# Hybrid SSD + S5 decoder step on one core: S5 coefficient and rotation products moved from GpSimd to VectorE, S5 state split into two 64-row halves

## The chip, the cores and the metric

The kernel runs on one core of one Trainium2 chip. The metric is the device time of one execution in microseconds, the lower the better. The kernel before was timed in three runs.

## The reference, cut to what matters

One decoder layer is computed for 1024 prompt tokens and 8 samples of 4 tokens (1056 columns in all). The input is normed and projected; one half of the projection feeds a Mamba-2 branch (SSD), the other an S5 branch; both are gated, joined by an output projection, and followed by a gate and a final norm. The change lies in the S5 branch, which has 64 groups of 16 channels, each driving a 64-dimensional complex diagonal state:

```python
delta = jnp.exp(log_dt)[:, None]
ab = exp(lambda * delta)                        # complex, per group and state
bb = ((ab - 1) / lambda) * b                    # complex input matrix
bu = einsum('btgh,gph->btgp', u, bb)
x  = associative_scan(x_t = ab * x_{t-1} + bu_t)   # from h0
y  = einsum('btgp,ghp->btgh', x_re, c_re) - einsum('btgp,ghp->btgh', x_im, c_im) + d * u
```

(In the reference the complex products are written out in real and imaginary parts.)

## The kernel before

All work is feature-major: 128 features on the partitions, the 1056 tokens in three chunks of 352 columns. `dense` (L159 to L169, its matmuls on L167) makes one 128-row tile of a projection as 8 blocks of 3 products each (high and low parts of weight and input), so 24 matmuls of 352 columns a chunk and 72 a tile. In the text these are the "dense matmuls". Weights come through one raw buffer `wr` and are split by ScalarE (L73) and VectorE (L76, `wl<-wr,wh`).

The S5 branch is made in two stages.

- **Coefficients** (`s5_coef_base` L306, `s5_coef_batch` L428). 16 batches of 4 groups. A batch makes three matrices in SBUF and stores them to DRAM in `md`: the output matrix `op` (c times powers of a: three VectorE operations of 128x576, L453 to L455), the input matrix `wt` (powers of a times b: three GpSimd operations of 128x512, L478 to L480, then four transposes `wp` on TensorE and a copy by ScalarE), and a Toeplitz matrix that goes from matmuls `kp` by a small VectorE operation `ks` through `kd` in DRAM into `md` (eight DMAs for four batches, L471, on SyncE's queue). `op`, `wt`, `ks` and `bs` have two buffers each. The batches are interleaved with the dense tiles of u, two a tile.
- **Scan** (`s5_batch` L633). 16 batches of 4 groups, that is 2 pairs. A batch loads `u8`, `mm` (its slice of `md`) and `h8`; TensorE makes the inputs `vr`, `vi` (64 output rows for each group, two groups side by side on 128 partitions, L650); a table of rotations `cr`, `sr` is the complex product of two small tables (`cmul` on L660: six operations of 128x256 on GpSimd, with `sst` as scratch); VectorE rotates `vr`, `vi`, runs four scans (L674), rotates back and writes the state `sst`. In `sst` a group has its real parts on partitions 0 to 63 and its imaginary parts on 64 to 127, while the scan has the two groups of a pair there, so four VectorE operations of 64x256 write it (L682, L686). TensorE then adds two products of 128 rows a group into `yp`: Toeplitz times u (L693) and `op` times state (L694); ScalarE applies gelu (L695). The batches are interleaved with the 12 convolution tiles (`conv_tile`, three VectorE operations `acc` of 128x1080 each) and the dt tile.

After that come the SSD stage (with z_b tiles as filler), z_a, the output projection, the GLU and the gate. The order of instructions on each engine is fixed when the kernel is built: the scheduler places them by a simulated timeline, so a change in one stage can move the dense matmuls of others. Each engine runs its own list strictly in order.

Of the kernel before, what the change touches and what calls it, by code (L numbers as in the profile page):

```python
# [7 lines left out]
F32 = mybir.dt.float32  # L8
# [16 lines left out]
CW = 352  # L25
# [9 lines left out]
def hymba_ssd_s5_kernel(  # L35
# [10 lines left out]
    s5h: bass.AP,  # L46
# [90 lines left out]
    md = dt_("md", 128, 64, 3, 128)  # L137
# [33 lines left out]
    # 1 / sqrt(mean of squares + eps) of the tokens of a chunk, on every partition  # L171
# [5 lines left out]
    def rstd_tok(sqs, n):  # L177
        """sqs: feature-major squares [128, CW]; the result [token, group of tokens]."""
        sp = psa("nsp")
        qt = sqs[0].shape[1] // 4  # L180
        for j in range(4):
            for i, q in enumerate(sqs):
                PE.matmul(out=sp[0:qt, j:j + 1], lhsT=q[:, qt * j:qt * j + qt], rhs=ones[:, 0:1],
                          start=(i == 0), stop=(i == len(sqs) - 1))
        v, y, t = (nw_p.tile([128, 4], F32, tag=q, name=q, bufs=b)[0:qt] for q, b in (("nv", 2), ("ny", 3), ("nt", 2)))
        ts(v, sp[0:qt, 0:4], 1.0 / n, EPS, ALU.mult, ALU.add)
        ts(y.bitcast(I32), v.bitcast(I32), 1, None, ALU.logical_shift_right)
        ts(y.bitcast(I32), y.bitcast(I32), -1.0, float(0x5F3759DF), ALU.mult, ALU.add)
        for _ in range(3):
            mul(t, v, y)  # L190
            stt(t, y, -0.5, t, ALU.mult, ALU.mult)
            stt(y, t, 1.5, y, ALU.add, ALU.mult)
        return y

    def rstd_bcast(y):
        """on every partition: a PSUM tile [128, CW]"""
        qt = y.shape[0]
        rb = psb("nrb")[:, 0:4 * qt]
        for j in range(4):
            PE.matmul(out=rb[:, qt * j:qt * j + qt], lhsT=y[:, j:j + 1].to_broadcast([qt, 128]),  # L200
                      rhs=ident[0:qt, 0:qt], start=True, stop=True)
        return rb

    def rstd_wide(y, n):
        """y, in place = 1 / sqrt(mean of y over n + 4 eps) on every partition; a Newton step polishes the root"""
        w = y.shape[1]
        sb, v = psb("nsb")[:, 0:w], ev("nv", w)
        PE.matmul(out=sb, lhsT=ones, rhs=y, start=True, stop=True)
        act(v, sb, AF.Identity, scale=1.0 / n, bias=eps4)
        act(y, v, AF.Ln)  # L210
        act(y, y, AF.Exp, scale=-0.5)
        mul(sb, v, y)
        stt(sb, sb, -0.5, y, ALU.mult, ALU.mult)
        stt(y, sb, 1.5, y, ALU.add, ALU.mult)
        return y
# [90 lines left out]
    def s5_coef_base():  # L306
# [57 lines left out]
        # rotation tables (partition = (g2, p), free = (pair, c))  # L364
# [9 lines left out]
        # a^4 h0 of the sample group  # L374
# [11 lines left out]
        # P[k] = a^k (rows 0-63), i a^k (rows 64-127), k = 0..8  # L386
# [13 lines left out]
        # f = (a - 1) / lambda  # L400
# [16 lines left out]
        # Z: f over -f  # L417
# [10 lines left out]
    def s5_coef_batch(b):  # L428
        cf, cf2, P, Z = cfc["p"], cfc["p2"], cfc["P"], cfc["Z"]
        g0, g1 = GB * b, GB * b + GB  # L430
        if b % 4 == 0:
            cfc["bc"] = row("bc")[:, 0:1024]
            for q2 in range(2):
                dma(out=cfc["bc"][64 * q2:64 * q2 + 64], in_=s5bc[:, b // 4])
            # b-bar (rows 0-63), minus b-bar (rows 64-127), re and im
            bn = cfc["bc"].rearrange("p (b t r x) -> p b t r x", b=4, t=2, r=2)[:, :, 0]
            zz = row("bz")[:, 0:1024].rearrange("p (r b g h) -> p r b g h", r=4, b=4, g=GB)
            n4 = lambda i: bn[:, :, i].rearrange("p b (g h) -> p b g h", h=16)
            f4 = lambda i: Z[:, i, g0:g0 + 16].rearrange("p (b g) -> p b g", b=4).unsqueeze(3).to_broadcast([128, 4, GB, 16])
            cmul(zz[:, 0], zz[:, 1], n4(0), n4(1), f4(0), f4(1), zz[:, 2], zz[:, 3])  # L440
            cfc["bz"] = zz
# [6 lines left out]
        # O[(ri, p), g, k, h] = (Re; -Im) of c a^k  # L448
# [7 lines left out]
        # rows 64-127 of P hold i a^k: Re(i c a^k) = -Im(c a^k)  # L456
        dms(out=md[:, g0:g1, 2], in_=op[:, :, 1:9].rearrange("p g k h -> p g (k h)"))
# [15 lines left out]
        # W[(s, h), g, (ri, p)] = (Re; Im) of a^(7-s) f b, built transposed  # L473
# [4 lines left out]
        mul(wt, x8(0), b8_(0), G)  # L478
        mul(w2, x8(1), b8_(1), G)
        sub(wt, wt, w2, G)  # L480
# [47 lines left out]
    def dt_tile():  # L528
# [11 lines left out]
        # w high | w low on 32 partitions; summed by the transposes to [token, chunk, head]  # L540
# [21 lines left out]
        # log1p(y) = ln(u) - ((u - 1) - y) / u with u = 1 + y rounded  # L562
# [6 lines left out]
        # sums over the tokens of a chunk or a sample row: up to each token, and of all of them  # L569
# [17 lines left out]
        # the 32 sample tokens three times over the partitions  # L587
# [45 lines left out]
    def s5_batch(b):  # L633
# [20 lines left out]
        sst = s5.tile([128, NB, 137], F32, tag="sst", name="sst")  # L654
        tc_, td = (sst.rearrange("p g c -> p (g c)")[:, 256 * i:256 * i + 256].rearrange("p (j c) -> p j c", c=128)
# [4 lines left out]
        cmul(v4(cr), v4(sr), b16(0), b16(1), b1(0), b1(1), v4(tc_), v4(td), G)  # L660
# [27 lines left out]
        yt = s51.tile([128, NB, 136], F32, tag="yt", name="yt")
# [10 lines left out]
    def ssd_mt(k, g, L, cb):  # L699
        """masked decay times C B, [s][head][l]"""  # L700
        mt = sdc["p"].tile([128, 8, 128], F32, tag="ab", name="ab", bufs=ABB)[0:L, :, 0:L]
        if k < 8:
            dma(out=mt, in_=acs_d[16 * k + 8 * g:16 * k + 8 * g + 8].partition_broadcast(L))
        else:
            dma(out=mt, in_=acs_s[8 * g:8 * g + 8].rearrange("e b s -> e (b s)").partition_broadcast(L))
        cbm = sdc["p"].tile([128, 128], F32, tag="cbm", name="cbm")[0:L, 0:L]
        mul(cbm, cb[0:L, 0:L], causal if k < 8 else cs[0:32, C_SMASK:C_SMASK + 32])
        for e in range(8):
            act(mt[:, e], mt[:, e], AF.Relu, scale=-1.0, bias=tok[0:L, 0, k, 8 * g + e:8 * g + e + 1])
        act(mt, mt, AF.Exp, scale=-1.0)  # L710
        mul(mt, mt, cbm.unsqueeze(1).to_broadcast([L, 8, L]))
        return mt
# [65 lines left out]
    def sample_prep():  # L778
# [3 lines left out]
        for g in range(2):  # L782
            # the 32 tokens three times over the partitions: high, high, low parts of B against high, low, high of x
# [77 lines left out]
    s5fin = cc.tile([128, 64], F32, name="s5fin")  # L861
# [158 lines left out]
    # scaled by the final norm and stored, while the next chunk is under way  # L1020
# [47 lines left out]
def _layout(i):  # L1068
# [15 lines left out]
    def tiles(w):  # L1084
# [30 lines left out]
    a["s5h"] = f(h.transpose(0, 3, 2, 1).reshape(128, 64, 8))  # L1115
# [17 lines left out]
         ("o_s5p", (128, 64)), ("o_s5s", (128, 2, 32, 8))]  # L1133


def _outputs(r):
# [9 lines left out]
    s5p = r["o_s5p"].reshape(2, 64, 64).transpose(0, 2, 1).reshape(2, 1, 1, 64, 64)  # L1146
# [18 lines left out]
```

## Time and profile before

| what | value |
|---|---|
| median of 3 runs | 1073.57 us (1072.02 to 1079.29) |
| profiled execution, span | 1074.0 us |
| mean granted TensorE clock | 0.972 |
| TensorE busy | 1018.8 us (95%) |
| VectorE busy | 760.1 us (71%) |
| ScalarE busy | 457.1 us (43%) |
| GpSimd busy | 307.0 us (29%) |

The span runs from the first to the last instruction. No other time of the profiled execution is given; its span is 0.4 us above the median of the runs, so that what lies around it is not told apart from the scatter of the runs, and sums made in the trace are read as times of a run. The matmuls overlap each other (one of 352 columns is shown as 0.32 us long, while the next starts 0.16 us later), so a busy TensorE is not a full one. The shares are means over stages that differ: by the slices of the page, VectorE is near 100% busy from about 110 to 200 us and from 275 to 430 us, and 30 to 50% in the last third.

### The profile page before, as it was taken

The page shows a single profiled execution, that of the slowest core. Times are in us where ns is not written, and L with a number is a line of the kernel's source. Part 1 is how long each engine was busy: PE and PEld are TensorE (multiplying, and loading weights), DVE is VectorE, ACT ScalarE, POOL GpSimd, SP SyncE. Part 2 cuts the span into 40 slices and gives each one's busy share as a digit, 9 for nine tenths or more (in the row PEclk, how much of TensorE's full clock was granted, in tenths as well). Part 3 has the DMA queues.
Part 4 walks back from the last instruction along what each step waited for, and adds up shares of the span by engine and source line. Part 5 has one row for each costly group of instructions (what it writes and reads, how often), then busy time and mean ns, then how long its engine had stood idle before and what let it go on. Part 6 is the DMA issues. An engine that isn't in the chain of part 4 may idle for free.

```text
span 1074.0 us, 17756 instructions
## 1 busy us (share of the span) xinstructions
PE 1018.8 (95%) x6608; PEld 962.8 (90%) x6608; DVE 760.1 (71%) x1460; ACT 457.1 (43%) x926; POOL 307.0 (29%) x385
## 2 busy tenths in 40 slices
PE   7999887899999989999999999999999999999995
PEld 7899776699989889987788899899999999999995
DVE  5779999776999999478789785667333334455466
ACT  7534134437444441575554567423233333324321
POOL 0600689643345433124443221000000002221221
PEclk9899998899999999999999999999999999999997
DMA  9526377652234455446653211698522322322232
GB/s 319 197 74 175 106 206 202 181 192 97 100 123 155 153 165 193 148 145 205 203 168 120 70 60 54 219 307 281 184 92 81 110 90 87 105 102 79 81 120 102
DMA packets 112486, 157.12 MB, mean 146 GB/s; under 512 B 13584, under 2 KB 88464, under 8 KB 112400
## 3 DMA queue, kind: packets, MB, share of 16 engines
q1 hardware_dynamic: 83376, 136.46, 39.2%
q10 hardware_dynamic: 29024, 19.54, 5.8%
q8 instruction: 52, 0.85, 0.3%
q14 instruction: 34, 0.28, 0.1%
HBM read 109.49 MB, written 50.67 MB: 149 GB/s over the span
## 4 chain that ended last, share of the span: by engine, by line
PE 47%; DVE 21%; DMA 8%; issue 5%; ACT 4%; SPq 1%; DVEq 0%; ACTq 0%
PE psd L167 40%; DVE acc L88 3%; DMA gr<-gd 2%; DVE sst L76 2%; DVE ta L76 2%; DVE tb L76 2%; DVE wl L76 2%; DMA hp_d<-xl 1%; DVE ui L674 1%; DVE op L76 1%; ACT L73 1%; DVE ur L674 1%; DMA wr<-wall 1%; PE yd L717 1%; DVE x L88 1%
## 5 line engine op out<-in xcount | busy, mean ns | idle before, releaser
L167 PE MATMUL psd<-n_h,wh 128*128 128x352 f32 x864 | 289.4, 335 | 0.4 <-DVE zt L88 0.4
L167 PE MATMUL psd<-n_h,wl 128*128 128x352 f32 x864 | 288.5, 335 | 0.0
L167 PE MATMUL psd<-n_l,wh 128*128 128x352 f32 x864 | 287.4, 333 | 0.0
L167 PEld LDWEIGHTS psd<-n_h,wh 128*128 128x128 f32 x864 | 166.6, 193 | 6.5 <-issue 3.6
L167 PEld LDWEIGHTS psd<-n_l,wh 128*128 128x128 f32 x864 | 166.6, 193 | 5.4 <-issue 4.6
L167 PEld LDWEIGHTS psd<-n_h,wl 128*128 128x128 f32 x864 | 166.1, 192 | 5.9 <-issue 5.5
L76 DVE TENSOR_TENSOR wl<-wr,wh 128x1024 fp32r<-128x1024 f32 (+1 forms) x64 | 81.7, 1277 | 46.4 <-ACT wh L73 45.6
L73 ACT ACTIVATE wh<-wr 128x1024 fp32r<-128x1024 f32 (+2 forms) x65 | 67.0, 1031 | 87.3 <-PE psd L167 78.3
L76 POOL TENSOR_TENSOR ssq<-ssq,xl 128x352 f32<-128x352 f32 x21 | 21.5, 1024 | 276.9 <-ACT xl L73 276.9
L76 POOL TENSOR_TENSOR sst<-r,r 128x256 f32<-128x256 f32 x64 | 52.0, 834 | 72.0 <-PE yp L694 41.5
L167 PE MATMUL psd<-ya_h,wh 128*128 128x352 f32 x192 | 63.5, 333 | 6.8 <-DVE xl L76 6.5
L73 ACT ACT_TABLE_LOAD x39 | 50.0, 1283 | 37.1 <-DVE acc L88 30.8
L73 ACT ACTIVATE ab<-ab,tok 128x128 f32<-128x128 f32 (+1 forms) x144 | 42.8, 380 | 49.2 <-DMA ab<-acs_d 29.7
L167 PE MATMUL psd<-ya_l,wh 128*128 128x352 f32 x192 | 63.3, 330 | 0.0
L167 PE MATMUL psd<-ya_h,wl 128*128 128x352 f32 x192 | 63.2, 330 | 0.0
L167 PE MATMUL psd<-yb_l,wh 128*128 128x352 f32 x192 | 62.2, 324 | 0.0
L167 PE MATMUL psd<-yb_h,wl 128*128 128x352 f32 x192 | 62.0, 323 | 0.0
L167 PE MATMUL psd<-g_l,wh 128*128 128x352 f32 x192 | 61.8, 322 | 0.0
L167 PE MATMUL psd<-g_h,wh 128*128 128x352 f32 x192 | 61.8, 322 | 0.0
L167 PE MATMUL psd<-g_h,wl 128*128 128x352 f32 x192 | 61.8, 322 | 0.0
L167 PE MATMUL psd<-yb_h,wh 128*128 128x352 f32 x192 | 61.7, 321 | 0.0
L167 PE MATMUL psd<-hg_h,gwl 128*128 128x400 f32 (+1 forms) x144 | 46.7, 324 | 0.0
(315 smaller groups left out, 2350.9 us busy)
## 6 DMA issues: line engine op xcount, KB each, us to landing
wr<-wall SPq DMA_DIRECT2D x68, 512.0 KB, 3.3
mm<-md SPq DMA_DIRECT2D x16, 768.0 KB, 6.2
ab<-acs_d SPq DMA_DIRECT2D x16, 512.0 KB, 4.5
ud<-ub ACTq DMA_DIRECT2D x8, 576.0 KB, 3.7
u<-ud SPq DMA_DIRECT2D x16, 288.0 KB, 3.3
gd<-yt SPq DMA_DIRECT2D x16, 272.0 KB, 4.4
gr<-gd SPq DMA_DIRECT2D x8, 544.0 KB, 5.1
x<-xT SPq DMA_DIRECT2D x24, 176.0 KB, 5.3
```

The source lines that it names most:

```text
L73: return S.activation(out=out, in_=in_, func=func, **kw)
L76: return (eng or V).tensor_tensor(out=out, in0=a, in1=b, op=op)
L88: return V.scalar_tensor_tensor(out=out, in0=a, scalar=s, in1=b, op0=op0, op1=op1)
L167: PE.matmul(out=ps, lhsT=a[:, ko + k, :], rhs=b, start=(i == 0), stop=(i == 3 * K - 1))
L674: V.tensor_tensor_scan(out=u[:, j], data0=cb["mag8"][:, j0 + j:j0 + j + 1].to_broadcast([128, 128]), data1=u[:, j], initial=0.0, op0=ALU.m ...
L717: PE.matmul(out=yd[64 * (e % 2):64 * (e % 2) + 64, e // 2], lhsT=x1[:, e], rhs=mt[:, e], start=True, stop=True)
```

## The change

- In `s5_coef_batch` the three `wt` operations of a batch run on VectorE instead of GpSimd.
- In `s5_batch` the six operations of `cmul` that make `cr`, `sr` run on VectorE instead of GpSimd.
- The state `sst` is kept as it comes from the scan: partitions are (half, p), the half being the group of the pair, and real and imaginary parts stand side by side in the free dimension. It is written by two VectorE operations of 128x256 instead of four of 64x256.
- The product `op` times state of a group becomes two matmuls of 64 rows (real, imaginary) on the half of the partitions where the group lies; the two groups of a pair use different halves and write different PSUM tiles. In fp32 each matmul is two instructions: a batch has 16 of 64 rows instead of 8 of 128 rows.
- `op` is stored in a DRAM tensor of its own, `od`, by four DMAs a batch instead of one (on ScalarE's queue), and loaded into its own tile `om`; `mm` shrinks from 768 to 512 KB. `h8` is loaded from `s5ha`, and the input `s5h` goes away. The layout of one output follows.

```diff
-    md = dt_("md", 128, 64, 3, 128)
+    md = dt_("md", 128, 64, 2, 128)
+    od = dt_("od", 2, 64, 32, 2, 128)
...
-        dms(out=md[:, g0:g1, 2], in_=op[:, :, 1:9].rearrange("p g k h -> p g (k h)"))
+        for q in range(2):
+            for ri in range(2):
+                dms(out=od[q, :, g0 // 2:g1 // 2, ri],
+                    in_=op[64 * ri:64 * ri + 64, q::2, 1:9].rearrange("p g k h -> p g (k h)"))
...
-        mul(wt, x8(0), b8_(0), G)
-        mul(w2, x8(1), b8_(1), G)
-        sub(wt, wt, w2, G)
+        mul(wt, x8(0), b8_(0))
+        mul(w2, x8(1), b8_(1))
+        sub(wt, wt, w2)
...
-        mm = s5.tile([128, NB, 3, 128], F32, tag="mm", name="mm")
+        mm = s5.tile([128, NB, 2, 128], F32, tag="mm", name="mm")
         dma(out=mm, in_=md[:, g0:g0 + NB])
-        tm, wv, om = mm[:, :, 0], mm[:, :, 1], mm[:, :, 2]
-        h8 = s5.tile([128, NB, 8], F32, tag="h8", name="h8")
-        dma(out=h8, in_=s5h[:, g0:g0 + NB])
+        tm, wv = mm[:, :, 0], mm[:, :, 1]
+        om = s5.tile([128, NJ, 2, 128], F32, tag="om", name="om")
+        dma(out=om, in_=od[:, :, j0:j0 + NJ].rearrange("q p j r c -> (q p) j r c"))
+        h8 = s5.tile([128, 2, NJ, 8], F32, tag="h8", name="h8")
+        dma(out=h8, in_=s5ha[:, :, j0:j0 + NJ])
...
-        cmul(v4(cr), v4(sr), b16(0), b16(1), b1(0), b1(1), v4(tc_), v4(td), G)
+        cmul(v4(cr), v4(sr), b16(0), b16(1), b1(0), b1(1), v4(tc_), v4(td))
...
-        for q in range(2):
-            sub(s2[0:64, :, q, 9:137], ta[64 * q:64 * q + 64], tb[64 * q:64 * q + 64])
+        sub(sst[:, 0, :, 9:137], ta, tb)
         mul(ta, ui, cr)
         mul(tb, ur, sr)
+        add(sst[:, 1, :, 9:137], ta, tb)
...
-        for h in range(NB // 2):
-            yp = psb("yp")[:, 0:272].rearrange("p (g c) -> p g c", c=136)
-            for i in range(2):
-                g = 2 * h + i
-                PE.matmul(out=yp[:, i], lhsT=tm[:, g], rhs=u8[:, g, 0:136], start=True, stop=False)
-                PE.matmul(out=yp[:, i], lhsT=om[:, g], rhs=sst[:, g, 0:136], start=False, stop=True)
-            act(yt[:, 2 * h:2 * h + 2], yp, AF.Gelu_apprx_tanh)
+        yp = [psb("yp")[:, 0:136 * NJ].rearrange("p (j c) -> p j c", c=136) for _ in range(2)]
+        for j in range(NJ):
+            for q in range(2):
+                g = 2 * j + q
+                PE.matmul(out=yp[q][:, j], lhsT=tm[:, g], rhs=u8[:, g, 0:136], start=True, stop=False)
+            for ri in range(2):
+                for q in range(2):
+                    hq = slice(64 * q, 64 * q + 64)
+                    PE.matmul(out=yp[q][:, j], lhsT=om[hq, j, ri], rhs=sst[hq, ri, j, 0:136], start=False, stop=(ri == 1))
+        for q in range(2):
+            act(yt[:, q::2], yp[q], AF.Gelu_apprx_tanh)
```

The order on the engines moves as follows. First VectorE in the coefficient stage, some batches in: `op`, `ra` are the output matrix and its scratch, `ks` belongs to the Toeplitz matrix. Before:

```order
L76 TENSOR_TENSOR op<-P,bc 128x576
L76 TENSOR_TENSOR op<-op,ra 128x576
L76 TENSOR_TENSOR ra<-P,bc 128x576
L88 SCALAR_TENSOR_TENSOR ks<-cs,dq,kp 128x16
L76 TENSOR_TENSOR op<-P,bc 128x576
L76 TENSOR_TENSOR op<-op,ra 128x576
```

And now, at the same place (`wt`, `rb` are the input matrix and its scratch):

```order
L75 TENSOR_TENSOR wt<-P,bz 128x512
L75 TENSOR_TENSOR ra<-P,bc 128x576
L75 TENSOR_TENSOR op<-P,bc 128x576
L75 TENSOR_TENSOR rb<-P,bz 128x512
L87 SCALAR_TENSOR_TENSOR ks<-cs,dq,kp 128x16
L75 TENSOR_TENSOR op<-op,ra 128x576
L75 TENSOR_TENSOR wt<-wt,rb 128x512
```

The three `wt` operations that were a list of GpSimd's stand between those of `op`, so that a batch is six large VectorE operations and `ks`.

Second TensorE in the scan stage, where the output of a batch is made. Before, between two dense matmuls (`L694` is `op` times state):

```order
L167 MATMUL psd<-n_h_112,wh 128x352
L694 MATMUL yp<-sst,mm 128x136
L693 MATMUL yp<-u_3383,mm 128x136
L694 MATMUL yp<-sst,mm 128x136 x2
L693 MATMUL yp<-u_3383,mm 128x136
L694 MATMUL yp<-sst,mm 128x136
L167 MATMUL psd<-n_l_120,wh 128x352
```

And now (`L701` is the 64-row product, `L655` the input of the next batch; an `x2` of `L701` is one for each half):

```order
L655 MATMUL vr<-u_3460,mm 64x136
L701 MATMUL yp<-sst,om 128x136 x2
L655 MATMUL vi<-u_3460,mm 64x136
L655 MATMUL vr<-u_3460,mm 64x136
L655 MATMUL vi<-u_3460,mm 64x136
L655 MATMUL vr<-u_3460,mm 64x136
L701 MATMUL yp<-sst,om 128x136 x2
L697 MATMUL yp<-u_3293,mm 128x136 x2
L701 MATMUL yp<-sst,om 128x136 x4
L655 MATMUL vi<-u_3460,mm 64x136
L655 MATMUL vr<-u_3460,mm 64x136
L655 MATMUL vi<-u_3460,mm 64x136
```

The output product of one batch has moved into the input product of the next, and matmuls of three array shapes (128 rows by 128 columns, 128 by 64, 64 by 128) take turns.

Third VectorE in the scan stage, the rotation of one batch now:

```order
L75 TENSOR_TENSOR ta<-vr,cr 128x256
L75 TENSOR_TENSOR tb<-vi,sr 128x256
L87 SCALAR_TENSOR_TENSOR acc<-b_3369,vc,acc 128x1080
L75 TENSOR_TENSOR cr<-sst 128x256
L75 TENSOR_TENSOR ur<-ta,tb 128x256
L87 SCALAR_TENSOR_TENSOR acc<-b_3369,vc,acc 128x1080
L75 TENSOR_TENSOR sst<-r_632,r_631 128x256 x2
L75 TENSOR_TENSOR ta<-vi,cr 128x256
```

The table for the next batch (`cr<-sst`, `sst<-r`, later `sr<-sst`) stands between the operations of the batch that is under way.

## Rows read from the trace of the kernel before

**Rows 1.** The page: span and busy time of each engine, then a weight split.

```profile
span 1074.0 us, 17756 instructions
...
PE 1018.8 (95%) x6608; PEld 962.8 (90%) x6608; DVE 760.1 (71%) x1460; ACT 457.1 (43%) x926; POOL 307.0 (29%) x385
...
L76 DVE TENSOR_TENSOR wl<-wr,wh 128x1024 fp32r<-128x1024 f32 (+1 forms) x64 | 81.7, 1277 | 46.4 <-ACT wh L73 45.6
```

**Rows 2.** Windows: busy PE, PEld, DVE, ACT, POOL; then granted clock, DMA share, GB/s.

```profile
118.00:221.00 103.00, 85.50 (x559) 71.87 (x559) 88.25 (x95) 35.96 (x94) 85.64 (x95) 0.88 0.67 195
221.00:275.00 54.00, 53.33 (x368) 50.19 (x366) 42.46 (x86) 32.88 (x58) 15.32 (x26) 1.00 0.30 100
275.00:439.00 164.00, 156.09 (x1091) 149.31 (x1088) 156.81 (x304) 65.79 (x118) 68.14 (x110) 0.97 0.45 151
```

**Rows 3.** Waits from 118 to 221 us: who waited for whom, us, times, longest.

```profile
PEld kp L460 <- issue: 15.6, 16, 3.4
PE kp L460 <- DVE op L76: 14.2, 7, 3.2
```

**Rows 4.** GpSimd's groups by form: count, busy us, mean ns, idle before.

```profile
L76 POOL TENSOR_TENSOR sst<-r,r 128x256 f32<-128x256 f32 x64 | 52.0, 834 | 72.0 <-PE yp L694 41.5 <-ACT s5fin L73 17.6 <-DMA md<-kd 6.5
L76 POOL TENSOR_TENSOR wt<-wt,rb 128x512 f32<-128x512 f32 x16 | 26.8, 1673 | 0.5
...
L76 POOL TENSOR_TENSOR wt<-P,bz 128x512 f32<-128x512 f32 x16 | 24.4, 1529 | 6.5 <-DVE P L76 6.0 <-PE wp L483 0.4
```

**Rows 5.** Tile op: duration ns min/median/max, first and last start.

```profile
L76 DVE TENSOR_TENSOR op<-P,bc x16: 746/1478/1701, 118.4 to 195.7; 128x576 f32<-128x576 f32 x16
L76 DVE TENSOR_TENSOR op<-op,ra x16: 757/1508/1728, 124.6 to 199.4; 128x576 f32<-128x576 f32 x16
L457 ACTq DMA_DIRECT2D md<-op x16: 366/366/398, 126.4 to 201.0; - x16
```

**Rows 6.** VectorE's groups by form: the small ks, then an uncontended 128x512.

```profile
L88 DVE SCALAR_TENSOR_TENSOR ks<-cs,dq,kp 128x16 f32<-128x16 f32 x16 | 3.4, 220 | 1.0 <-PE kp L460 1.0
...
L76 DVE TENSOR_TENSOR x<-xt,tok 128x512 f32<-128x512 f32 x16 | 10.9, 683 | 4.3 <-PE xt L755 2.8 <-DMA gd<-yt 1.3
```

**Rows 7.** Tile mm: duration ns, first and last start of inputs and outputs.

```profile
L650 PE MATMUL vr<-u,mm x128: 279/279/330, 220.8 to 426.6; 128*64 128x136 f32 x128
...
L694 PE MATMUL yp<-sst,mm x128: 277/279/434, 234.3 to 438.6; 128*128 128x136 f32 x128
```

**Rows 8.** VectorE's groups by form from 295 to 395.3 us, eight scan batches.

```profile
L76 DVE TENSOR_TENSOR sst<-ta,tb 64x256 f32<-64x256 f32 x32 | 13.5, 421 | 0.8
...
L674 DVE TENSOR_TENSOR_SCAN ui<-mag,ui 128x128 f32<-128x128 f32 x16 | 9.9, 658 | 0.2
...
L76 DVE TENSOR_TENSOR ui<-ta,tb 128x256 f32<-128x256 f32 x8 | 5.5, 690 | 0.0
```

**Rows 9.** Tile ui: durations of the scan and the sum, ns min/median/max.

```profile
L674 DVE TENSOR_TENSOR_SCAN ui<-mag,ui x32: 397/724/899, 226.4 to 432.2; 128x128 f32<-128x128 f32 x32
L76 DVE TENSOR_TENSOR ui<-ta,tb x16: 393/776/898, 226.0 to 431.4; 128x256 f32<-128x256 f32 x16
```

**Rows 10.** Timeline of TensorE in the SSD stage: start, us; a 64-row product.

```profile
563.14 0.32 PE L167 MATMUL psd<-n_l,wh 128*128 128x352 f32 x1
563.30 0.32 PE L167 MATMUL psd<-n_h,wl 128*128 128x352 f32 x1
563.55 1.07 PE L832 MATMUL yos<-cs,ys 64*128 64x32 f32 x8
564.56 0.43 PE L167 MATMUL psd<-n_h,wh 128*128 128x352 f32 x1
```

**Rows 11.** Timeline of TensorE at 426 us: column halves of two groups.

```profile
426.23 0.33 PE L650 MATMUL vi<-u,mm 128*64 128x136 f32 x2
426.34 0.28 PE L650 MATMUL vr<-u,mm 128*64 128x136 f32 x1
426.39 0.28 PE L650 MATMUL vi<-u,mm 128*64 128x136 f32 x1
```

More of the change, by code (lines that the diff above doesn't have):

```diff
@@ L653, in s5_batch @@
         cr, sr, ta, tb = (mk(p, n) for p, n in ((s5, "cr"), (s5, "sr"), (s51, "ta"), (s51, "tb")))
-        sst = s5.tile([128, NB, 137], F32, tag="sst", name="sst")
-        tc_, td = (sst.rearrange("p g c -> p (g c)")[:, 256 * i:256 * i + 256].rearrange("p (j c) -> p j c", c=128)
+        sst = s5.tile([128, 2, NJ, 137], F32, tag="sst", name="sst")
+        tc_, td = (sst.rearrange("p r j c -> p (r j c)")[:, 256 * i:256 * i + 256].rearrange("p (j c) -> p j c", c=128)
                    for i in range(2))
@@ L675, in s5_batch @@
                                      data1=u[:, j], initial=0.0, op0=ALU.mult, op1=ALU.add)
-        G.tensor_copy(out=sst[:, :, 0:8], in_=h8)
-        G.memset(sst[:, :, 8:9], 0.0)
-        s2 = sst.rearrange("p (j q) c -> p j q c", q=2)
+        G.tensor_copy(out=sst[:, :, :, 0:8], in_=h8)
+        G.memset(sst[:, :, :, 8:9], 0.0)
         mul(ta, ur, cr)
         mul(tb, ui, sr)
-        for q in range(2):
-            sub(s2[0:64, :, q, 9:137], ta[64 * q:64 * q + 64], tb[64 * q:64 * q + 64])
+        sub(sst[:, 0, :, 9:137], ta, tb)
         mul(ta, ui, cr)
         mul(tb, ur, sr)
-        for q in range(2):
-            add(s2[64:128, :, q, 9:137], ta[64 * q:64 * q + 64], tb[64 * q:64 * q + 64])
-        act(s5fin[:, g0:g0 + NB], sst[:, :, 136])
-        yt = s51.tile([128, NB, 136], F32, tag="yt", name="yt")
-        for h in range(NB // 2):
-            yp = psb("yp")[:, 0:272].rearrange("p (g c) -> p g c", c=136)
-            for i in range(2):
-                g = 2 * h + i
-                PE.matmul(out=yp[:, i], lhsT=tm[:, g], rhs=u8[:, g, 0:136], start=True, stop=False)
-                PE.matmul(out=yp[:, i], lhsT=om[:, g], rhs=sst[:, g, 0:136], start=False, stop=True)
-            act(yt[:, 2 * h:2 * h + 2], yp, AF.Gelu_apprx_tanh)
+        add(sst[:, 1, :, 9:137], ta, tb)
+        act(s5fin[:, :, j0:j0 + NJ], sst[:, :, :, 136])
+        yt = s51.tile([128, NB, 136], F32, tag="yt", name="yt")
+        yp = [psb("yp")[:, 0:136 * NJ].rearrange("p (j c) -> p j c", c=136) for _ in range(2)]
[7 more added lines that the diff above has]
+                    PE.matmul(out=yp[q][:, j], lhsT=om[hq, j, ri], rhs=sst[hq, ri, j, 0:136], start=False, stop=(ri == 1))
+        for q in range(2):
+            act(yt[:, q::2], yp[q], AF.Gelu_apprx_tanh)
         dma(out=gd[:, :, g0:g0 + NB].rearrange("t h g c -> (t h) g c"), in_=yt)
@@ L860, in hymba_ssd_s5_kernel @@
                     r16=cc.tile([128, 2, 32, 8], F32, name="r16"), a4h=cc.tile([128, 2, 32, 8], F32, name="a4h"))
-    s5fin = cc.tile([128, 64], F32, name="s5fin")
+    s5fin = cc.tile([128, 2, 32], F32, name="s5fin")
     bt, ct, xs = [None, None], [None, None], [None] * 8
@@ L1132 @@
 _OUTS = [("o_y", (8, 128, T)), ("o_ssdp", (128, 1024)), ("o_ssds", (8, 128, 1024)), ("o_conv", (128, 12, 27)),
-         ("o_s5p", (128, 64)), ("o_s5s", (128, 2, 32, 8))]
+         ("o_s5p", (128, 2, 32)), ("o_s5s", (128, 2, 32, 8))]
 def _outputs(r):
@@ L1145, in _outputs @@
     ss = r["o_ssds"].reshape(8, 128, 16, 64).transpose(0, 2, 3, 1).reshape(1, 8, 16, 64, 128)
[L1146 removed]
+    s5p = r["o_s5p"].reshape(2, 64, 2, 32).transpose(2, 3, 0, 1).reshape(2, 1, 1, 64, 64)
     s5s = r["o_s5s"].reshape(2, 64, 2, 32, 8).transpose(2, 4, 3, 0, 1).reshape(2, 1, 8, 64, 64)
```

2 lines of the change are left out of this document (removed).

## The prediction

> **What bounds the kernel now.** I read the page first for shares, then the windows of the two S5 stages, then the waits in them, then single tiles for durations, and last the timeline of TensorE for what lies between two matmuls. The page shows TensorE busy for 95% of the span and GpSimd for 29% [rows 1]; the bound changes from stage to stage, so I price the change where it is made.
>
> In the coefficient stage (118 to 221 us) VectorE is busy for 88.25 of 103 us, and both it and GpSimd are near full until 200 us; TensorE waits [rows 2]. Its largest waits are for `kp`, 14.2 us for VectorE's `op` and 15.6 us more before its weight load [rows 3]. In the scan, from 275 us on, VectorE is busy 156.81 of 164 us and TensorE 156.09 [rows 2]: both are nearly full. Between the two, from 221 to 275 us, TensorE is full (53.33 of 54) and VectorE has air (42.46).
>
> VectorE is as full as it is because GpSimd slows it. `op<-P` of 128x576 takes 746 ns at best and 1478 in the median, `op<-op` 757 and 1508 [rows 5]. The scan takes 397 ns at best and 724 in the median, the sum `ui` 393 and 776 [rows 9]; these are the operations that run while GpSimd works on `wt` or on the rotation tables [rows 4].
>
> **The change, part by part.**
>
> *Coefficients on VectorE.* Before, a batch costs VectorE three operations of about 1.48 us and 0.22 for `ks`, 4.7 us [rows 5, 6], while GpSimd works 1.53 to 1.67 us on each of its three [rows 4]. Now VectorE has three of 0.75 (the best ones of before) and three of 128x512. No such product of two SBUF tiles stands uncontended in the rows; the nearest is a 128x512 product with one PSUM input, 0.68 us [rows 6]. From both sides: 0.6, scaled from 746 ns for 576 elements, to 0.75; I take 0.68. That is 2.25 + 2.04 + 0.22 = 4.51 us, hardly less than before: what GpSimd's silence gives back pays for its work. Sixteen batches are 72.2 us, and three weight splits stand between them at 1.28 [rows 1], so 76.0. VectorE starts at about 116 instead of 118.4 (the powers of a are built beside a quiet GpSimd) and ends at 192. Before, the last `op<-op` starts at 199.4 and ends at 200.9, and the first `vr` starts at 220.8 [rows 5, 7]: 19.9 us for the last `ks`, the store to `kd`, the eight loads and stores on SyncE's queue and the load of `mm`. This tail stays as it is (the load of `om` stands behind `mm` and isn't needed for `vr`), so `vr` starts at 212, which is 8.8 us earlier.
>
> *What TensorE owes then.* The order says what has been done by that point. Before, 960 dense matmuls stand ahead of the first `vr`, now 864: a convolution tile and a third has gone behind it. A dense matmul takes 0.16 us, the distance of two starts [rows 10]. At the last output of the scan it is 1864 before and 1825 now. So in the scan TensorE makes 961 instead of 904, 57 more or +9.1 us, and the 39 left over cost 6.2 us after it, where TensorE is again close to full.
>
> *Scan on VectorE.* A batch gets six operations of 128x256 for the tables. Such a size is about 0.42 us (that is what 64x256 takes [rows 8], and it is the elements in a partition that count), so +2.51 us. The state is written by two operations instead of four, -0.84. The four scans fall from 0.66 to 0.40, -1.04, and `ui` from 0.69 to 0.39, -0.30 [rows 8, 9]; `ur` and the first `ta` have less of the same, an estimate of -0.3 together. Sum 0.0 us: VectorE does as much as before.
>
> *Output product in halves.* A batch has 16 instructions of 64 rows for 8 of 128. If the two halves of a pair run side by side, this costs nothing; if one after the other, eight more at 0.115 us (two column-half streams of 136 columns start 0.11 apart in pairs [rows 11]) are 0.92 us a batch, 14.7 us in all. What the trace shows is that column halves do run in pairs: four starts in 0.23 us [rows 11]. Row halves of two tiles it doesn't show. I take nothing, and keep 14.7 for the range. The Trainium skill, in "TensorEngine Tiling (Array Packing)" under Key Properties, says that different tiles load weights and multiply in parallel, and under Gotcha 1 that row tiles must write different PSUM banks; by it the sum is as I take it, since the halves write two tiles.
>
> *Changes of shape.* This is a cost that I do charge. A dense matmul is followed by the next after 0.16 us, but by a 64-row one after 0.25; and after eight of those (seven steps of 0.11 in the 1.07 us) the next dense one starts about 0.23 us behind the last, so about 0.09 to 0.11 each way [rows 10]. TensorE's list changes its array shape 125 times before and 209 times now, since the 64-row products stand between the 64-column ones. 84 at 0.09 are +7.6 us. The same page says under Key Properties that changing the mode drains the engine; the trace agrees, with those 0.09 us.
>
> *What TensorE can win back.* In the scan it is idle for 0.7 + 7.9 = 8.6 us, and the clock of 0.97 over 164 us is another 4.9 [rows 2]: 13.5 us in which it waited for VectorE or ran slowly after waiting. With 16.7 us more to do it will fill most of these; I take two thirds, -9.0. It can't have all, because the order ties the engines more tightly: the output of one batch now stands inside the input of the next, and the tables stand on VectorE's list where they wait for the scratch in `sst`.
>
> *Queues.* ScalarE issues four stores of `op` for one, at 0.37 us each [rows 5], +1.1 us a batch; `om` adds a load a batch on SyncE. ScalarE is busy for 36 of 103 us in the stage [rows 2], so I cost both at nothing; without that cover, below.
>
> *Sum.* -8.8 (earlier `vr`) + 9.1 (57 dense) + 7.6 (shapes) - 9.0 (filled waits) + 6.2 (39 dense later) = +5.1 us. On the span of 1074.0 this is 1079.1; the span stands within 0.5 us of the median 1073.57, and I make nothing of that difference. Forecast 1079, a small loss that a measurement can hardly tell from no change (1% of the median, 10.7 us, is about what it can tell).
>
> **The rivals.**
>
> *The row halves run one after the other.* Place: the 16 output products. Price 14.7 us on a TensorE that is full, 1079 + 15 = 1094, slower. It decides once TensorE has no more idle time in the scan than the 8.6 us of before. For it: no row shows row halves at once. Against: column halves run at once [rows 11], and the order puts the two halves next to each other.
>
> *ScalarE becomes the bound of the coefficients.* `op` has two buffers; its third use waits until all four stores of the first have landed, and ScalarE, in strict order, issues 2.2 us of stores and others a batch, beside its copies. If half of the added 17.6 us (16 x 1.1) shows, 1088. For it: `op` now comes round every 4.5 us. Against: ScalarE has two thirds of its time free [rows 2].
>
> *VectorE was the true bound, and gains.* If its batches run closer than the sum of durations (72.2 us become 66), `vr` starts 6 us earlier; if in the scan all 13.5 us of idle time go, 4.5 more; if the changes of shape hide in what waits are left, 7.6 more: 1061. For it: VectorE is at 96% from 275 us on. Against: from 221 to 275 it had air, and TensorE was full [rows 2].
>
> *It does nothing in effect:* the work only changes place, 1074.
>
> **How the numbers follow.** Forecast (1079, give or take 6) 0.45; halves in turn 0.15; ScalarE 0.17; VectorE's gain 0.13; nothing 0.10. Faster by over 1% (below 1062.8) holds most of VectorE's case, 0.11. Slower by over 1% (above 1084.3) holds the halves, three quarters of ScalarE's case and a tenth of the forecast's, 0.32. The rest is 0.57. The range runs from just above the end of VectorE's case to the halves with a little beside them: 1063 to 1096; the forecast's own is 1073 to 1085.
>
> **What would show it.** Right: `op` and `ra` at 0.75 us, `wt` near 0.68 on VectorE; scans at 0.40; the first `vr` at 206 to 214 us; a busy TensorE from there to the last output, at about 438 us; pairs of 64-row products starting within 20 ns of each other; 0.09 us at each change of shape. Wrong: a first `vr` at or after 220 (ScalarE or the stores of `op` hold VectorE); 64-row products 0.115 us apart each (halves in turn); VectorE idle in the scan while it waits for `vr`, or `wt` well above 0.75; and a stage after the scan that takes the 39 matmuls into gaps at no cost, which would take the sum to 1073.

## The result and the profile after

| | median | range | ratio to before |
|---|---|---|---|
| before | 1074.14 us | 1072.02 to 1079.29 (4 runs) | |
| changed kernel | 1102.41 us | 1095.91 to 1105.25 (4 runs) | 1.0249 [1.0217, 1.0282] |

The change makes the kernel 2.5% slower. The forecast was 1079 with a range up to 1096. The profiled execution of the changed kernel is the fastest of the four (1095.91 us, span 1094.1), so its trace shows 20.1 us of the loss; the other 8 lie in runs without a trace.

The page of the changed kernel, beside [rows 1]:

```profile
span 1094.1 us, 18048 instructions
...
PE 1026.7 (94%) x6736; PEld 960.0 (88%) x6736; DVE 738.5 (67%) x1572; ACT 462.8 (42%) x929; POOL 158.8 (15%) x241
```

GpSimd has lost half of its work, and VectorE, which took it over, is busy for 22 us less than before. So VectorE did not pay. The windows show where the time went (columns as in [rows 2]), the coefficient stage first, then its worst 40 us, then the scan:

```profile
118.00:217.00 99.00, 67.39 (x464) 57.18 (x463) 72.95 (x127) 30.39 (x84) 5.26 (x37) 0.78 0.72 192
...
150.00:160.00 10.00, 5.07 (x41) 3.62 (x39) 10.00 (x18) 2.52 (x8) 0.85 (x6) 0.80 0.83 217
160.00:170.00 10.00, 4.45 (x28) 2.55 (x28) 9.96 (x19) 3.49 (x10) 0.55 (x4) 0.50 0.73 187
170.00:180.00 10.00, 2.35 (x20) 1.11 (x20) 8.77 (x16) 1.85 (x7) 0.60 (x4) 0.50 0.76 194
180.00:190.00 10.00, 3.40 (x24) 1.84 (x24) 5.27 (x10) 2.46 (x8) 0.61 (x4) 0.50 0.83 214
...
275.00:451.00 176.00, 176.00 (x1247) 159.58 (x1246) 142.40 (x335) 78.88 (x131) 12.70 (x40) 1.00 0.43 138
```

In the coefficient stage TensorE is busy for 67.39 of 99 us where it had 85.50 of 103 [rows 2]; from 160 to 190 us it works 10 us of 30, and after the half-idle stretch ahead of that (5.07 of 10) the granted clock is 0.50, its lower level of 1.2 GHz. From 275 us to the end of the scan it is busy without a gap, while VectorE has 34 us of air. Before, both were near full there.

Why TensorE stands idle is read from the tiles and waits. Tile `op` (columns as in [rows 5]; an indented line gives the idle time of an engine before its operations on the tile, what ended it, and how often; here the engine is VectorE):

```profile
L459 ACTq DMA_DIRECT2D od<-op x64: 582/614/1814, 121.5 to 198.7; - x64
L75 DVE TENSOR_TENSOR op<-P,bc x16: 747/758/761, 116.8 to 192.4; 128x576 f32<-128x576 f32 x16
L75 DVE TENSOR_TENSOR op<-op,ra x16: 746/754/759, 120.7 to 193.2; 128x576 f32<-128x576 f32 x16
...
  DMA od<-op: 12.0, 7
```

Tile `wt`, now made on VectorE, in the same columns; the idle time here is that of TensorE, before the transposes that read `wt`:

```profile
L75 DVE TENSOR_TENSOR wt<-P,bz x16: 678/685/693, 112.9 to 178.5; 128x512 f32<-128x512 f32 x16
...
  ACT wo L72: 32.5, 11
```

And a scan of tile `ui`, to be laid beside [rows 9]:

```profile
L680 DVE TENSOR_TENSOR_SCAN ui<-mag,ui x32: 394/407/426, 224.2 to 442.2; 128x128 f32<-128x128 f32 x32
```

All VectorE prices came out as forecast: `op` 0.75, `wt` 0.685, the scans 0.41 us. But each store of half rows takes ScalarE's queue 0.614 us, where the one store of before took 0.366 [rows 5]: 4 x 0.614 = 2.46 us a batch, not 1.46. VectorE waits 12.0 us until `op` has been stored. TensorE waits 32.5 us, weight loads and products together, for ScalarE's copy `wo`, which stands in the same list as the stores. The waits from 122 to 217 us show ScalarE's own wait and the weight loads' part of TensorE's (us, times, longest):

```profile
ACT ks L72 <- DMA od<-op: 21.5, 6, 5.2
PEld wp L486 <- ACT wo L72: 18.6, 6, 3.9
```

Last the scan, on TensorE's timeline, where an output product stands inside the next input product (start, duration from the first start to the last end, count):

```profile
382.50 0.45 PE L655 MATMUL vr<-u,mm 128*64 128x136 f32 x2
382.78 0.39 PE L655 MATMUL vi<-u,mm 128*64 128x136 f32 x2
383.10 0.50 PE L701 MATMUL yp<-sst,om 64*128 64x136 f32 x4
...
384.58 0.73 PE L697 MATMUL yp<-u,mm 128*128 128x136 f32 x4
385.24 0.73 PE L701 MATMUL yp<-sst,om 64*128 64x136 f32 x8
```

Eight 64-row products take as long as four of 128 rows: the halves run side by side. But four 64-row products alone take 0.50 us, more than half of that. And the first two `vr` and two `vi` above start one by one, 0.12 to 0.17 us apart; before, the column halves of two groups ran in pairs [rows 11]. Of the 256 starts of `vr` and `vi`, 158 were followed by another within 0.08 us before, and 116 are now.

### The profile page after: what moved, and what is told of

Same layout as the page of the kernel before. It is cut to its first block, busy times and chain, and to the rows that moved or that the text cites. A ratio compares the mean times of both kernels' runs of the same rounds, so it can differ in the third digit from the quotient of the medians.

```text
span 1094.1 us, 18048 instructions
## 1 busy us (share of the span) xinstructions
PE 1026.7 (94%) x6736; PEld 960.0 (88%) x6736; DVE 738.5 (67%) x1572; ACT 462.8 (42%) x929; POOL 158.8 (15%) x241
## 4 chain that ended last, share of the span: by engine, by line
PE 64%; DMA 7%; DVE 6%; ACT 3%; issue 2%; POOL 0%; DVEq 0%; ACTq 0%
PE psd L167 51%; DMA gr<-gd 3%; PE yp L701 2%; PE yp L697 2%; PE yd L725 1%; DVE zr L87 1%; PE vr L655 1%; PE vi L655 1%; ACT L72 1%; PE st L777 1%; DMA wr<-wall 1%; DVE x L87 1%; DMA hb<-h0T 1%; PE psd L548 1%; PE yo L774 1%
## 5 line engine op out<-in xcount | busy, mean ns | idle before, releaser
L167 PE MATMUL psd<-n_h,wl 128*128 128x352 f32 x864 | 284.8, 331 | 0.0
L75 DVE TENSOR_TENSOR wl<-wr,wh 128x1024 fp32r<-128x1024 f32 (+1 forms) x64 | 78.8, 1232 | 69.8 <-ACT wh L72 68.9
L72 ACT ACTIVATE wh<-wr 128x1024 fp32r<-128x1024 f32 (+2 forms) x65 | 67.2, 1034 | 106.6 <-PE psd L167 93.4
L72 ACT ACT_TABLE_LOAD x42 | 53.9, 1283 | 11.9 <-DVE acc L87 8.1
L167 PE MATMUL psd<-hg_h,gwh 128*128 128x400 f32 (+1 forms) x144 | 46.6, 323 | 0.0
```

The source lines that it names most:

```text
L72: return S.activation(out=out, in_=in_, func=func, **kw)
L75: return (eng or V).tensor_tensor(out=out, in0=a, in1=b, op=op)
L167: PE.matmul(out=ps, lhsT=a[:, ko + k, :], rhs=b, start=(i == 0), stop=(i == 3 * K - 1))
```

## The experiments

Three views are worked out from each trace and used below: the dense matmuls between the first `wp` and the first `vr` (coefficients), up to the last `yp` (scan), up to the last SSD product, and after it; and "S5 starts", the sum, over all `vr`, `vi` and `yp` matmuls, of the distance to TensorE's next start, waits included. A dense matmul at full clock takes 0.16 us [rows 10].

| kernel | median us | dense: coefficients, scan, SSD, rest | first vr | last yp | S5 starts us |
|---|---|---|---|---|---|
| before | 1074.1 | 343, 904, 506, 2718 | 220.8 | 438.6 | 48.6 |
| changed | 1102.4 | 231, 961, 507, 2756 | 216.1 | 450.5 | 67.2 |
| products on VectorE alone | 1072.5 | 518, 1029, 286, 2622 | 220.2 | 444.8 | 47.8 |
| halves and four stores | 1112.1 | 175, 999, 502, 2795 | 223.4 | 462.7 | 63.4 |
| change with one store | 1063.3 | 513, 812, 522, 2608 | 221.2 | 428.2 | 60.3 |
| change, products bundled | 1087.2 | 231, 971, 522, 2731 | 219.5 | 444.9 | 58.8 |
| one store, bundled | 1064.4 | 513, 842, 480, 2620 | 220.4 | 429.9 | 57.2 |
| change, stores on SyncE | 1068.6 | 570, 794, 479, 2612 | 229.3 | 434.9 | 61.5 |
| four stores alone | 1100.0 | 175, 1051, 525, 2720 | 223.3 | 458.6 | 54.5 |
| products, four stores | 1076.3 | 231, 996, 510, 2718 | 217.1 | 438.5 | 47.7 |
| `wt` on VectorE alone | 1070.4 | 518, 881, 432, 2624 | 220 | 434 | 49.7 |
| tables on VectorE alone | 1072.3 | 343, 1030, 469, 2629 | 218 | 440 | 46.1 |
| halves alone, one store | 1088.7 | 338, 836, 502, 2795 | 219 | 438 | 65.7 |
| one store, three tiny ones | 1087.6 | 217, 975, 507, 2756 | 207.8 | 441 | 64.4 |

**Products on VectorE alone.** Before, with these lines:

```diff
-        mul(wt, x8(0), b8_(0), G)
+        mul(wt, x8(0), b8_(0))
...
-        cmul(v4(cr), v4(sr), b16(0), b16(1), b1(0), b1(1), v4(tc_), v4(td), G)
+        cmul(v4(cr), v4(sr), b16(0), b16(1), b1(0), b1(1), v4(tc_), v4(td))
```

> Only the products move to VectorE (both sets, wt and cr/sr); the state, the output product and the single store of op stay as before. Theory S (the four stores of op for one fill ScalarE's queue and starve the coefficient stage): the loss is gone, 1055 to 1075 us, first vr preceded by 1151 dense matmuls. Theory H (the 64-row products and the changes of array shape cost the time in the scan): the loss is gone too, same number. Theory V (VectorE can't carry the products, the loss is its load): still slow, 1090 to 1105.

Measured 1072.51, ratio 0.9989 [0.9969, 1.0009]: VectorE loses nothing, which rules out Theory V; S and H forecast the same number, so this run doesn't part them. The order now puts 518 dense matmuls into the coefficient stage, and TensorE is full there; but 220 fewer are left for the SSD stage, which goes idle. Windows of this kernel (columns as in [rows 2]):

```profile
120.00:220.00 100.00, 100.00 (x720) 90.78 (x718) 88.17 (x155) 48.49 (x113) 11.60 (x41) 1.00 0.72 203
...
460.00:600.00 140.00, 119.35 (x820) 89.97 (x819) 116.80 (x206) 76.93 (x210) 58.70 (x52) 0.91 0.46 139
```

The same two windows of the kernel before:

```profile
120.00:220.00 100.00, 82.50 (x539) 69.09 (x538) 86.29 (x91) 35.38 (x92) 83.63 (x92) 0.88 0.67 195
460.00:600.00 140.00, 138.41 (x992) 114.20 (x991) 118.36 (x212) 73.48 (x204) 56.54 (x50) 1.00 0.53 165
```

17.5 us more of busy TensorE in the first window, 19 less in the second: a gain given back.

**Halves and four stores, products on GpSimd.** The changed kernel with the diff above undone.

> Only the state halves, the 64-row products, the four stores and the separate load of om; the products stay on GpSimd. Theory S: slow by the coefficient stage, 1090 to 1105, with od issues of about 0.6 us each and a ScalarE queue that never rests there. Theory H: slow by the scan alone, about 1074 + 19 = 1093, with a first vr no later than 221 us. Theory V: no loss, 1065 to 1078.

Measured 1112.12, ratio 1.0345 [1.0324, 1.0366]. The loss stays, and grows above the range of each theory, without any work moved to VectorE.

**The change with one store.** `od` in the layout of `op`, loaded by four small DMAs on SyncE:

```diff
-        for q in range(2):
-            for ri in range(2):
-                dms(out=od[q, :, g0 // 2:g1 // 2, ri],
-                    in_=op[64 * ri:64 * ri + 64, q::2, 1:9].rearrange("p g k h -> p g (k h)"))
+        dms(out=od[:, g0:g1], in_=op[:, :, 1:9].rearrange("p g k h -> p g (k h)"))
...
-        dma(out=om, in_=od[:, :, j0:j0 + NJ].rearrange("q p j r c -> (q p) j r c"))
+        odv = od.rearrange("(r p) (j q) c -> q p j r c", r=2, q=2)
+        for q in range(2):
+            for j in range(NJ):
+                dma(out=om[64 * q:64 * q + 64, j], in_=odv[q, :, j0 + j])
```

> The whole change, but op is stored by one DMA of 128 partitions as before, and om loaded by four small DMAs on SyncE's queue instead of one. Theory S: most of the loss goes, 1065 to 1080, and TensorE is fed during the coefficients. Theory H: the loss of the scan stays, about 19 us of the 28, so 1088 to 1098. Theory V: unchanged, about 1100.

Measured 1063.34, ratio 0.9894 [0.987, 0.9917]: faster than both kernels, and 39 us faster than the change. Its windows, to be laid beside those of the change:

```profile
120.00:220.00 100.00, 100.00 (x721) 90.84 (x720) 88.03 (x156) 48.38 (x113) 12.24 (x40) 1.00 0.70 198
...
460.00:600.00 140.00, 135.98 (x947) 110.98 (x945) 112.90 (x203) 72.49 (x188) 62.40 (x53) 0.99 0.47 151
```

The coefficient stage ends no earlier (`vr` at 221.2), but 282 more dense matmuls are done by then.

**The change with the products bundled.** For each pair the imaginary product first, so that the order keeps the output product of a batch together:

```diff
-            for ri in range(2):
+            for ri in (1, 0):
```

> The whole change, with the imaginary half of the output product ahead of the real one, so that no 64-row product is ready before the whole state is, and TensorE's list has 176 changes of array shape instead of 209. Theory S: about the same as the change, 1095 to 1103. Theory H: 33 changes at 0.09 us and the input products back in pairs, 8 to 15 us less than the change, 1085 to 1095. Theory V: unchanged.

Measured 1087.16, ratio 1.0114 [1.0088, 1.0141]. Same coefficient stage, S5 starts 58.8 instead of 67.2: the mixing of the two products, with the few dense matmuls that move along, is 15 us of the loss (the two traces, 1085.4 and 1094.1, show 8.7 of it). On the timeline eight 64-row products now stand together, and `vr` and `vi` come in fours again:

```profile
379.88 0.45 PE L655 MATMUL vi<-u,mm 128*64 128x136 f32 x4
380.26 0.73 PE L701 MATMUL yp<-sst,om 64*128 64x136 f32 x8
380.93 0.73 PE L697 MATMUL yp<-u,mm 128*128 128x136 f32 x4
```

**One store and bundled.** Both edits.

> The whole change with op stored by one DMA a batch (as in the one-store run) and, for each pair, the imaginary product issued before the real one (as in the run that did only that). If the two costs are separate, they add: the one-store run took 39.1 us off the change (1102.4 to 1063.3) and the other order of the products 15.2 (1102.4 to 1087.2), so 1048. If the second gain was only the filling of a stage that the one store now fills by itself, nothing is added: 1063. Expected 1053, between the two, and below the kernel before in either case.

Measured 1064.35, ratio 0.991 [0.9892, 0.9928]: the gains don't add. With one store the bundling shortens the S5 starts by only 3.1 us (60.3 to 57.2), not by 8.4. The SSD stage has 480 dense matmuls instead of 522; that this takes back the 3 us is likely, but was not tested.

**The four stores on SyncE's queue.** `dms` becomes `dma` in the four stores of the change.

> The whole change with its four stores of op a batch, but issued on SyncE's queue instead of ScalarE's. Theory A (what costs is ScalarE's strict list: 4 x 0.61 us a batch in the coefficient stage, by which copies come late and by which the scheduler's order puts only 231 dense matmuls between the first wp and the first vr): ScalarE is free again, the order now has 570 there (1203 ahead of the first vr), TensorE is full from 120 to 220 us at full clock, and the time falls to that of the one-store run, 1063, give or take 8. Theory B (four 64-row stores are dear wherever they are issued, by their number or because the two buffers of op wait for all of them): it stays near the change, 1090 to 1105, with TensorE idle between 150 and 200 us.

Measured 1068.64, ratio 0.9947 [0.9931, 0.9963]. Theory A: the same four DMAs cost nothing like 28 us on another engine's list. The Trainium skill ("Perfetto Trace Analysis", DMA Optimizations) says that balancing DMAs over the engines that can issue them may help where descriptor generation is the bottleneck. The outcome of this run agrees, 1068.6 for 1102.4; what the issue time is spent on, no run shows.

**The four stores alone.** The kernel before, with one edit:

```diff
-        dms(out=md[:, g0:g1, 2], in_=op[:, :, 1:9].rearrange("p g k h -> p g (k h)"))
+        for q in range(2):
+            for ri in range(2):
+                dms(out=md[64 * ri:64 * ri + 64, g0 + q:g1:2, 2],
+                    in_=op[64 * ri:64 * ri + 64, q::2, 1:9].rearrange("p g k h -> p g (k h)"))
```

> The kernel before with one edit: the store of op into md in four DMAs of 64 rows on ScalarE's queue instead of one; products stay on GpSimd, state and output product as before. Theory A: the stores alone make it slower. The order has 792 dense matmuls ahead of the first vr instead of 960; at 0.16 us each, with a first vr that stays at 220 us, these 168 cost 27 us: 1101, range 1088 to 1112. Rival (the 64-row halves and the changes of shape cost most of the loss, the stores little): 1074 to 1080.

Measured 1100.03, ratio 1.0246 [1.0222, 1.027]. This one edit, costed at nothing in the prediction, loses as much as the whole change. The window of the coefficient stage:

```profile
120.00:220.00 100.00, 54.65 (x348) 43.64 (x349) 67.53 (x65) 23.00 (x72) 77.77 (x89) 0.66 0.66 174
```

**Products on VectorE and four stores.** Both edits in the kernel before.

> The kernel before with the products on VectorE (as in the run that did only that, 1072.5) and the store of op in four DMAs of 64 rows on ScalarE's queue; state and output product as before. Theory A: 864 dense matmuls ahead of the first vr, 96 fewer than before, +15 us on 1074: 1089, range 1082 to 1100; the same count as the whole change has, so that the rest up to its 1102, some 13 us, is what the halves cost in the scan. Rival (the stores are only dear together with the halves): 1073.

Measured 1076.28, ratio 1.002 [1.0004, 1.0035], 13 us better than expected and near the rival's 1073. The coefficient stage is as idle as that of the change, which has 6.80 and 10.88 us of busy TensorE in these two windows:

```profile
160.00:180.00 20.00, 7.67 (x58) 3.88 (x56) 19.35 (x33) 5.26 (x16) 1.15 (x8) 0.50 0.73 193
180.00:200.00 20.00, 10.72 (x64) 8.28 (x64) 8.02 (x15) 5.40 (x18) 1.09 (x7) 0.55 0.82 216
```

Yet nearly nothing is lost, as the scan took 92 dense matmuls more than before in only 4 us more (221.4 for 217.8); TensorE, which stood idle for 8.6 us there before, is now nearly full. So the count ahead of the first `vr` alone does not give the time. With the same 864 ahead of it, the change adds only the halves, and takes 26 us more (19 between the two traces): in the scan 35 fewer dense matmuls take 13 us longer, with S5 starts of 67.2 instead of 47.7.

**`wt` alone, tables alone.** Half of the first diff each.

> The kernel before with the three wt operations on VectorE alone; rotation tables stay on GpSimd, op is stored by one DMA, state and output product as before. Theory F (dense matmuls are a filler that three stages share; one put into idle TensorE time of the coefficient stage is won, as long as the SSD stage keeps enough of them): 1151 dense matmuls stand ahead of the first vr instead of 960, with a first vr still at 220 us, the scan has 881 for 904 and some 4 us less, the SSD stage some 430 for 506 and 3 us less, the rest 94 fewer and 6 us less (that many were worth 6 us in the run with both products): 13 us less, 1061, range 1053 to 1068. Rival (VectorE pays for what it takes over, wherever the filler goes): no gain, 1071 to 1080.

Measured 1070.35, ratio 0.9974 [0.9955, 0.9994], a miss, next to the rival's range: the coefficients gain as expected, but the SSD stage with 432 dense matmuls takes 163 us, 5 more than before, instead of 3 less.

> The kernel before with the six operations of the rotation tables on VectorE alone; the wt operations stay on GpSimd, op is stored by one DMA, state and output product as before. Theory F: the coefficient stage is as before (960 dense matmuls ahead of the first vr, which stays at 221 us); the scan has 1030 dense for 904 and ends at about 446, +7 us, with VectorE's scans near 0.40 us; 6 to 8 us of this come back after the scan, which has 126 fewer to do: 1073, range 1066 to 1080. Rival (the tables on VectorE relieve a scan stage that VectorE bounds): the scan stays at 218 us with the 126 more in it, and the time falls by some 10 us, to 1063.

Measured 1072.34, ratio 0.9978 [0.996, 0.9996]: the number of Theory F to within 1 us, but in part by luck. The scan ended at 440, not 446, and with 126 more dense matmuls (20 us at 0.16) it took 4 us more, between the 7 of Theory F and the none of the rival. Windows of this kernel, and of the one before:

```profile
300.00:380.00 80.00, 80.00 (x574) 77.57 (x574) 77.96 (x177) 41.75 (x67) 8.53 (x22) 1.00 0.46 157
```

```profile
300.00:380.00 80.00, 75.17 (x523) 71.66 (x523) 77.73 (x148) 34.53 (x60) 34.84 (x56) 0.96 0.41 137
```

VectorE did hold TensorE back there before; with GpSimd quiet, TensorE is full, and VectorE no longer bounds the scan.

**Halves alone, one store.** The one-store run with all products on GpSimd.

> The kernel before with the 64-row state and output product alone: all products on GpSimd as before, op stored by one DMA, om loaded by four small DMAs on SyncE's queue. Theory H (64-row products and changes of shape lengthen TensorE's list in the scan by 9 to 19 us, 57 to 67 for 48.6 us from start to start in the runs with halves): coefficient stage as before (955 dense ahead of the first vr), 836 dense for 904 in the scan, the scan about as long as before, 213 to 220 us, and 77 dense more after it at 0.16: +12 us, 1086, range 1076 to 1094. Rival (without the four stores the halves cost nothing, as the one-store run with 1063 against 1072 for the products alone suggests): 1065 to 1074.

Measured 1088.65, ratio 1.0148 [1.0118, 1.0177], Theory H. S5 starts are 65.7 us, and what the scan has no room for lies behind it.

**One store and three tiny ones.** The one-store run, and

```diff
+        for q in range(3):
+            dms(out=jd[b:b + 1, q], in_=op[q:q + 1, 0, 1])
```

> The one-store run (1063.3) with three more stores a batch on ScalarE's queue, of 64 bytes each (16 numbers of op into a scratch tensor that nothing reads); all else as in the one-store run. With them the scheduler lays out the order of the whole change again: 850 dense matmuls ahead of the first vr (one store 1146, the change 864), 1825 ahead of the last yp (1958, 1825). Theory O (the order is the cause: the scheduler holds ScalarE to be full and so puts too few dense matmuls into the coefficient stage): it takes the time of the change, 1100, range 1092 to 1106, with TensorE idle and at a lower clock from 150 to 200 us, though the op stores together issue for less than 2.46 us a batch. Theory Q (the chip's own queue is the cause: copies and stores come late behind four big stores): the tiny stores cost little to issue, and the time lies at 1063 to 1075 in spite of the order.

Measured 1087.55, ratio 1.0102 [1.0073, 1.0131]: between the theories. The tiny stores are not free (tile `op` of this kernel):

```profile
L460 ACTq DMA_DIRECT2D jd<-op x48: 221/325/1106, 123.3 to 193.1; - x48
...
L458 ACTq DMA_DIRECT2D od<-op x16: 366/388/1507, 122.9 to 190.9; - x16
```

A batch issues its stores of `op` for 0.39 + 3 x 0.33 = 1.36 us instead of 2.46. With nearly the order of the change, 24 of the 39 us that four stores lose against one are lost again, and the other 15 are not. The windows show the same idle TensorE as in the change, though `vr` starts 8 us sooner:

```profile
160.00:180.00 20.00, 8.50 (x60) 4.54 (x60) 19.90 (x35) 6.30 (x20) 1.52 (x10) 0.50 0.76 216
180.00:200.00 20.00, 12.00 (x64) 10.31 (x65) 7.61 (x15) 7.52 (x20) 0.82 (x5) 0.67 0.81 222
```

So two things act together: an order that puts 217 to 231 dense matmuls where 513 find room, and the chip's own queue, by which copies come late. The queue's part is about 15 us (7 between the two traces). The other 24 us belong to the order together with the 1 us a batch that the tiny stores take; this run doesn't part the two.

**What the parts cost, side by side.** Medians, us:

| | one store | four stores on ScalarE |
|---|---|---|
| as before | 1074 | 1100 |
| products on VectorE | 1072 | 1076 |
| halves | 1089 | 1112 |
| both | 1063 | 1102 |

The stores cost between 4 and 39 us, the halves between -9 and +26, according to what stands beside them. No part has a price of its own; each edit lays out the dense matmuls of four stages anew, as the counts show.

## Why the prediction was wrong

**Two steps failed: "Queues" and "Changes of shape".** "Queues" took each store at the 0.37 us of the one before, and costed four at nothing since ScalarE is busy for 36 of 103 us. A store of half the rows issues for 0.614, and a share of busy time is no cover on a list that runs strictly in order: the copy `wo`, the small `ks` and the evacuation of the u tiles stand behind the stores. TensorE waits for `wo` and the u tiles, SyncE for `kd` (47.2 us, before 36.4), and VectorE until the stores have landed. The rival "ScalarE becomes the bound" named the mechanism, but with half of 17.6 us it was priced too low: the one-store run puts it at 39, with the order that goes with it.

"Changes of shape" took the halves to cost 84 changes at 0.09 us, 7.6 in all; the S5 starts grew by 18.6. In the prediction's own sum, which goes by the order of the change, this is the larger miss: 11.0 of the 15.0 us between its +5.1 and the +20.1 of the trace. The queue shows there as 4.1 us at the first `vr`. The run with the products and four stores bears this out: the same idle coefficient stage without the halves takes 1076.3.

**What the order owed to the stores was not seen.** The prediction counted rightly what the order moves (864 dense matmuls ahead of `vr` for 960, 1825 for 1864 in all) and charged 15.3 us. It took this as given. One store brings the 864 to 1146. And 864 alone costs little, as the run with the products and four stores shows.

**Term by term,** for the 20.1 us that the profiled execution shows:

| term | predicted | measured | from |
|---|---|---|---|
| first `vr` | -8.8 | -4.7 | 216.1 for 220.8 |
| 57 dense in the scan | +9.1 | +9.1 | 961 for 904, at 0.16 |
| changes of shape | +7.6 | +18.6 | S5 starts 67.2 for 48.6 |
| filled waits | -9.0 | -11.1 | what is left of the scan's 234.4 for 217.8 |
| after the scan | +6.2 | +8.2 | 20.1 less 11.9 at the last `yp` |

*First `vr`.* VectorE ends at 194.0 (last `op<-op`, 193.2 and 0.75), close to the 192 of the sum. But the tail is 22.1 us instead of 19.9, with stores of `op` issued until 198.7 in the list that issues `kd`. With tiny stores, 1.36 us a batch instead of 2.46, `vr` starts at 207.8, within the forecast of 206 to 214.

*Changes of shape.* The price of one step was right: from a 128-row to a 64-row product takes 0.209 us and an unchanged step 0.115, so 0.09 each, 84 times. But a block of 64-row products has a second slow step: its second pair starts 0.21 us behind the first, a later one 0.11 behind the one ahead. With 48 blocks that is 4.9 us. The eight products that the price was read from [rows 10] are of one half, and the trace has no such step in them (0.13, then 0.11). Of the 18.6 us, 14.9 lie in the output products (44.6 for 29.7), with two waits of TensorE that make 2.5, and 3.9 in `vr` and `vi` (22.8 for 18.9), whose pairs are broken up. The prediction showed this very order, and counted in it only the changes. Bundling, with 32 blocks of eight, brings S5 starts to 58.8, where the term would have been +10.2.

*Right:* the durations on VectorE, the halves that run at once (against the rival "in turn"), the full TensorE in the scan, and the waits won back, 11.1 of 13.5 where two thirds were taken (a remainder, so it carries the errors of the other rows). That VectorE does as much in the scan as before was not right: it is busy for 188.3 us between the first `vr` and the last `yp`, before 199.3. "VectorE was the true bound" is half of the truth: the contention did vanish, and with one store 1063 is near what that rival gave (1061). That is luck in part: the rival had an earlier `vr` (it stays at 221.2), and the gain comes with 170 more dense matmuls in the coefficient stage.

**Open.** The 8 us between the profiled execution and the median of the changed kernel. The scheduler's reason to fill the coefficient stage or not was only argued from its orders; that the stores on ScalarE's list set it off is shown by four runs (one store, SyncE, four alone, tiny ones). Why the halves cost 26 us beside four stores, 15 alone, and gain 9 beside one store with the products on VectorE, is told here by the counts, and not shown by a run of its own. `om` is loaded by four DMAs in the runs with one store; what that costs alone wasn't tried.

## What to carry to other kernels

Count a DMA as an instruction of the engine that issues it, at the duration of its own shape, and look at what stands behind it on that list before calling it covered. Where filler is placed by a scheduler, compare the count of filler by stage before and after each small edit; a gain in one stage that takes the cover of the next is given back there, and an idle stage costs little where a later one has room for its filler. Try the parts of a change apart, and in pairs: here the good parts were hidden behind one layout of a store.

## What the runs showed that was not expected

- A store of 64 partitions (64 KB) holds ScalarE's queue for 0.614 us, one of all 128 partitions (256 KB) for 0.366 to 0.388, and one of 64 bytes still for 0.325.
- On SyncE's queue the same four stores take as long to issue (0.605 us in the median), and the kernel with them there takes only 5 us more than the one with one store.
- Row halves run at once: eight 64-row products in 0.73 us, as four of 128 rows, with the two starts of a pair 0.007 us apart. A block of four takes 0.50 us, since the second pair of a block starts 0.21 us behind the first and later ones 0.11. So a block of eight costs less than two of four.
